# Four weight splits moved to GpSimd and one norm queued ahead of the other half's transposes, in a one-core decoder layer

## The chip, the cores and the metric

The kernel runs on one core of a Trainium2 chip. A core has TensorE (PE, with its weight loads shown as PEld), VectorE (DVE), ScalarE (ACT), GpSimd (POOL) and SyncE (SP, which here only starts loads). The metric is the device time of one execution in microseconds. A name like L73 is line 73 of the kernel.

## What is computed

One layer of a decoder trunk for 256 tokens of width 2048, in float32. A token mixer is followed by an output projection; then comes a gated MLP with a width-3 causal convolution. Both have an RMS norm before and behind them and are scaled and shifted by a conditioning vector. The change lies between the output projection `merged @ w_o` and the up-projection `h @ w_up`:

```python
def rms_norm(x, g):
    y = x * lax.rsqrt(jnp.mean(x * x, axis=-1, keepdims=True) + RMS_EPS)
    return y * g

y = hybrid_mixer(h, ...)                       # ends with  merged @ w_o
x = x + gt1[:, None] * rms_norm(y, g_post_mix)
h = rms_norm(x, g_pre_ffn) * (1.0 + sc2[:, None]) + sh2[:, None]
up = causal_dwconv(h @ w_up, ffn_conv_w)       # w_up: 2048 x 11264
a, b = jnp.split(up, 2, axis=-1)
y = (jax.nn.silu(a) * b) @ w_down
x = x + gt2[:, None] * rms_norm(y, g_post_ffn)
```

## The kernel before

Every product is made from split operands: a value becomes hi (its rounding to fp32r, the format that TensorE takes) and lo (the value less hi). `split` (L71) does this with a cast on ScalarE (L72) and a subtraction on VectorE (L73). Weights come as tiles of 128x1024 in a fixed order, `sources` (L85): `weights` (L75) starts the load of one tile into `raw` (4 buffers) and splits it into `hi` and `lo` (4 buffers each; the last two tiles of the output projection go to `dx` buffers). `next_weights` (L121) hands out a tile and keeps two more on the way. What is written to a buffer waits until the buffer's last reader is through.

The output projection is `out_proj` (L270). It makes four column blocks n of 512, for two token halves t of 128 tokens each. In the last block the last six weight tiles are held, so that all products of half 0 come first, then all of half 1. Behind each half stand its square sum on ScalarE (L299), the product with the gate on VectorE (L300), and then `tail(t)`, which here is `mid` (L850), in a high-priority section. After half 0 one tile of the up-projection is prefetched, after half 1 the next ones.

`mid(t)` has two steps. The norm: `rms_scale` (L262) sums the four partial sums (reduction L264, square root on ScalarE L265, reciprocal L266, three Newton operations L258 to L260, all on 128x1 values); four operations add the result to x (L855, 128x512 each), each followed by a square sum on ScalarE (L856); a second `rms_scale`; and then the identity matrix is scaled by the second norm into `dg` (L859). The transposes: for four blocks b, four products of x with `dg` (L864) turn 128x128 pieces into a PSUM tile `tps` (of four PSUM buffers), two of the four pieces are scaled and shifted from PSUM by VectorE (L872), two by ScalarE (L874), and two splits write `h2p`, the operand of the up-projection, hi and lo side by side.

The up-projection loops over 44 column tiles f, twice each (the halves a and b): 16 products of `hi` with both parts of `h2p` (L901) and 16 of `lo` with the hi part (L902). It needs all of `h2p`, tile after tile.

The order on each engine is made by a scheduler from the order of the code, the priorities and the waits; each engine then works through its own list in that order. In the kernel before, GpSimd has work in the first 130 us only.

Of the kernel before, what the change touches and what calls it, by code (L numbers as in the profile page):

```python
# [49 lines left out]
def kernel(  # L50
# [3 lines left out]
    nc = tc.nc  # L54
    wmod_h = (wmod_h0, wmod_h1)
    wmod_t = (wmod_t0, wmod_t1)
    pool = lambda n, bufs=1, **kw: ctx.enter_context(tc.tile_pool(name=n, bufs=bufs, **kw))
# [6 lines left out]
    def raw_tile(src):  # L64
        t = sp.tile([P, 1024], F32, tag="raw", name="raw", bufs=4)
        nc.sync.dma_start(t, src)
        return t
# [3 lines left out]
    def split(src, hi, lo):  # L71
        marks["act"] = nc.scalar.copy(hi, src)  # L72
        nc.vector.tensor_sub(lo, src, hi)  # L73

    def weights(src, pool=None):  # L75
        r = raw_tile(src)
        if pool is None:
            h = sp.tile([P, 1024], F32R, tag="hi", name="hi", bufs=4)
            l = sp.tile([P, 1024], F32R, tag="lo", name="lo", bufs=4)
        else:  # L80
            h, l = (pool.tile([P, 1024], F32R, tag="dx", name="dx", bufs=5) for _ in range(2))
        split(r, h, l)
        return h, l

    def sources():  # L85
        for grp in GROUPS:
            for b in range(10):
                for g in grp:
                    yield wA[b, g], None
        for i in range(4):  # L90
            for f in (4 + i, 8 + i, i):
                for j in range(2):
                    yield wB[f, j], None
        for br in GATE_ORDER:
            for f in range(16):
                for j in range(2):
                    yield wB[12 + 16 * br + f, j], None
                if f % 2 == 0:
                    yield wbr[br, f // 2], None
        for n in range(4):  # L100
            for j in range(8):
                yield wo[n, j], marks["dx"] if n == 3 and j >= 6 else None
        for f in range(NF):
            for ft in (f, f + NF):
                for j in range(2):
                    yield wup[ft, j], None
        for n in range(4):
            for j in range(NF // 2):
                yield wdn[n, j], None

    queue = []
    stream = sources()

    def prefetch(n):
        while len(queue) < n:
            src = next(stream, None)
            if src is None:
                break
            queue.append(weights(*src))
# [137 lines left out]
    def newton(r, t, ms, n=1):  # L257
        nc.vector.scalar_tensor_tensor(t, r, -0.5 / n, r, ALU.mult, ALU.mult)  # L258
        nc.vector.scalar_tensor_tensor(ms, ms, EPS * n, t, ALU.add, ALU.mult)
        nc.vector.scalar_tensor_tensor(r, ms, 1.5, r, ALU.add, ALU.mult)  # L260

    def rms_scale(ss):  # L262
        v, t, r = (cp.tile([P, 1], F32, tag=n, name=n, bufs=2) for n in ("rv", "rt", "rr"))
        nc.vector.tensor_reduce(v, ss, AX.X, ALU.add)  # L264
        nc.scalar.activation(r, v, AF.Sqrt, bias=eps[:, 0:1], scale=1.0 / D)  # L265
        nc.vector.reciprocal(r, r)  # L266
        newton(r, t, v, D)
        return r
# [38 lines left out]
    with ExitStack() as mx:  # L307
# [275 lines left out]
        for gi, grp in enumerate(GROUPS):  # L583
# [3 lines left out]
            for b in range(10):  # L587
# [6 lines left out]
                for half in range(2):  # L594
                    ps = psA.tile([P, 2, S], F32, tag="A", name="inps")
                    if b < 7:
# [10 lines left out]
                        f = 0.125 if 1 <= b <= 3 else 1.0  # L607
                    else:
# [12 lines left out]
                        f = 1.0  # L621
# [39 lines left out]
        def glu(zp):  # L661
            gq, gqh, gql = ssm_st["g"]
            branch_tiles(0)
            wg = [weights(wglu[j]) for j in range(2)]
            for f in range(4):
                ps = psB.tile([P, 512], F32, tag="B", name="glups")
                for kt in range(4):
                    w = wg[kt // 2]
                    c = 512 * (kt % 2) + P * f
                    mm3(  # L670
                        ps[:, :S], w[0][:, c : c + P], w[1][:, c : c + P], gqh[:, kt], gql[:, kt],
                        kt == 0, kt == 3,
                    )
                sg = zp.tile([P, S], F32, tag="z", name="sg", bufs=2)
                nc.scalar.activation(
                    sg, ps[:, :S], AF.Sigmoid, bias=V[:, V_BGLU + f : V_BGLU + f + 1]
                )
                nc.vector.tensor_mul(sg, sg, gq[:, f])
                split(sg, bo_h[0][:, f], bo_l[0][:, f])
# [167 lines left out]
            pp.tile([P, 2, 2, S], F32R, tag="big", name="h2p", bufs=12) for _ in range(8)  # L847
        ]

        def mid(t):  # L850
            r = rms_scale(ss[:, t])
            s2 = cp.tile([P, 4], F32, tag="s2", name="s2", bufs=2)
            for n in range(4):
                y = yg1[n][:, t]
                nc.vector.scalar_tensor_tensor(x1[t][n], y, r[:, 0:1], x1[t][n], ALU.mult, ALU.add)  # L855
                nc.scalar.activation(y, x1[t][n], AF.Square, accum_out=s2[:, n : n + 1])  # L856
            r2 = rms_scale(s2)
            dg = mp.tile([P, P], F32, tag="uv", name="dg", bufs=20)
            nc.vector.tensor_scalar_mul(dg, ident, r2[:, 0:1])  # L859
            tk = slice(P * t, P * t + P)  # L860
            for b in range(4):
                ps = psB.tile([P, 4, P], F32, tag="B", name="tps")
                for i in range(4):
                    nc.tensor.matmul(  # L864
                        ps[:, i], x1[t][b][:, P * i : P * i + P], dg, start=True, stop=True
                    )
                h2 = mp.tile([P, 4, P], F32, tag="uv", name="h2", bufs=20)
                for i in range(4):
                    kt = 4 * b + i
                    sc, sh = scale2[:, kt : kt + 1], shift2[:, kt : kt + 1]  # L870
                    if i < 2:
                        nc.vector.tensor_scalar(h2[:, i], ps[:, i], sc, sh, ALU.mult, ALU.add)  # L872
                    else:
                        nc.scalar.activation(h2[:, i], ps[:, i], AF.Identity, bias=sh, scale=sc)  # L874
                for i in range(2):
                    hp = h2p[2 * b + i]
                    split(h2[:, 2 * i : 2 * i + 2], hp[:, :, 0, tk], hp[:, :, 1, tk])

        out_proj(
            KT // 2, lambda kt, tk: (mh[kt // 2][:, kt % 2, tk], ml[kt // 2][:, kt % 2, tk]),  # L880
            gg, ss, lambda n, t: yg1[n][:, t], mid, mg, 6,
        )

# [7 lines left out]
    for f in range(NF):  # L891
# [13 lines left out]
        for a in range(2):  # L905
            ft = f + NF * a
# [145 lines left out]
```

## Time and profile before

| | |
|---|---|
| runs | 1638.06, 1642.01, 1641.61 us; median 1641.61 |
| profiled execution | 1646.62 us, of which the span is 1644.6 |
| busy: PE, DVE, ACT, POOL | 1587.6 (97%), 1217.2 (74%), 814.7 (50%), 52.0 us (3%) |
| chain that ended last | PE 81%, DVE 8%, DMA 7%, ACT 3% |
| up-projection | from 892.2 us; PE busy throughout 900 to 1380 us |
| turn to the up-projection | last product of the output projection starts at 875.9 us |

Times in the rows are counted from the start of the span. A busy time is the sum of an engine's operations; an operation's start and its length are the first two columns of a timeline. The profiled execution is one single run, 5.0 us above the median; sums made from its rows are carried over to the median as differences.

### The profile page before, as it was taken

What the parts mean: (1) busy time and instruction counts of PE and PEld (TensorE: products, weight loads), DVE (VectorE), ACT (ScalarE), POOL (GpSimd) and SP (SyncE); (2) the same over time, 40 slices, a digit from 0 to 9 for tenths busy, and PEclk for the clock granted to TensorE, in tenths of its full rate; (3) what the DMA queues carried; (4) which work ended last, traced back from release to release, by engine and by line L of the source; (5) the groups of instructions that cost most, each with busy time, mean ns of one, the idle gap of its engine ahead of it and who ended that gap; (6) DMA issues with size and microseconds to landing.
All of it is one profiled execution on the core that took longest, in us unless ns stands there. A gap on an engine that the chain in (4) does not pass through costs nothing.

```text
span 1644.6 us, 26089 instructions
## 1 busy us (share of the span) xinstructions
PE 1587.6 (97%) x10112; PEld 1400.8 (85%) x10112; DVE 1217.2 (74%) x1854; ACT 814.7 (50%) x1223; POOL 52.0 (3%) x102
## 2 busy tenths in 40 slices
PE   5899999999999999999998999999999999999997
PEld 3898998889888889999887888888888888888886
DVE  5889987887777788787757778877788777444444
ACT  4553434664445554544446555555555555343342
POOL 8021000000000000000000000000000000000000
PEclk8899999999999999999999999999999999999999
DMA  7988975777776665888864777767777665556563
GB/s 264 367 316 281 372 264 172 252 252 251 266 269 240 211 230 165 299 304 321 291 200 137 227 238 235 232 215 231 235 236 230 201 190 188 185 191 191 187 188 125
DMA packets 107120, 388.52 MB, mean 236 GB/s; under 512 B 11890, under 2 KB 12018, under 8 KB 106996
## 3 DMA queue, kind: packets, MB, share of 16 engines
q1 hardware_dynamic: 105268, 380.96, 69.5%
q10 hardware_dynamic: 1728, 5.90, 1.0%
q8 instruction: 79, 1.29, 0.3%
q14 instruction: 45, 0.37, 0.1%
HBM read 384.71 MB, written 2.10 MB: 235 GB/s over the span
## 4 chain that ended last, share of the span: by engine, by line
PE 81%; DVE 8%; DMA 7%; ACT 3%; issue 2%; SPq 0%; DVEq 0%; ACTq 0%
PE ups L901 20%; PE ups L902 10%; PE ops L127 7%; PE ops L126 7%; PE ops L128 7%; PE gps L126 5%; PE gps L128 5%; PE gps L127 5%; PE inps L126 4%; PE inps L128 4%; PE inps L127 4%; DVE lo L73 3%; DMA raw<-in_wB 2%; DMA raw<-in_wmod_t 2%; DMA raw<-in_wA 1%
## 5 line engine op out<-in xcount | busy, mean ns | idle before, releaser
L73 DVE TENSOR_TENSOR lo<-raw,hi 128x1024 fp32r<-128x1024 f32 x520 | 635.4, 1225 | 290.1 <-ACT hi L72 287.8
L72 ACT CAST hi<-raw 128x1024 fp32r<-128x1024 f32 x520 | 543.0, 1047 | 555.2 <-PE ops L128 172.9
L901 PE MATMUL ups<-h2p,hi 128*128 128x512 f32 x1408 | 495.3, 394 | 0.1
L902 PE MATMUL ups<-h2p,lo 128*128 128x256 f32 x1408 | 398.1, 283 | 0.0
L901 PEld LDWEIGHTS ups<-h2p,hi 128*128 128x128 f32 x1408 | 264.4, 188 | 61.6 <-ACT hi L72 0.5
L902 PEld LDWEIGHTS ups<-h2p,lo 128*128 128x128 f32 x1408 | 264.7, 188 | 0.6 <-issue 0.5
L128 PE MATMUL gps<-hh,lo 128*128 128x256 f32 x768 | 217.2, 283 | 4.1 <-DVE lo L73 4.1
L126 PE MATMUL gps<-hh,hi 128*128 128x256 f32 x768 | 220.0, 286 | 0.2 <-ACT hi L72 0.2
L127 PE MATMUL gps<-hl,hi 128*128 128x256 f32 x768 | 216.8, 282 | 0.0
L126 PEld LDWEIGHTS gps<-hh,hi 128*128 128x128 f32 x768 | 145.5, 189 | 15.7 <-issue 8.9
L128 PEld LDWEIGHTS gps<-hh,lo 128*128 128x128 f32 x768 | 145.3, 189 | 4.9 <-DVE lo L73 4.9
L126 PE MATMUL inps<-hh,hi 128*128 128x256 f32 x448 | 128.1, 287 | 22.1 <-ACT hh L72 14.8
L127 PEld LDWEIGHTS gps<-hl,hi 128*128 128x128 f32 x768 | 145.4, 189 | 0.2 <-issue 0.2
L126 PE MATMUL ops<-hi,ah 128*128 128x512 f32 x352 | 138.9, 395 | 0.0
L127 PE MATMUL ops<-lo,ah 128*128 128x512 f32 x352 | 138.9, 395 | 0.0
L128 PE MATMUL ops<-hi,al 128*128 128x512 f32 x352 | 138.9, 395 | 0.0
L128 PE MATMUL inps<-hh,lo 128*128 128x256 f32 x448 | 128.2, 287 | 1.9 <-DVE lo L73 1.7
L127 PE MATMUL inps<-hl,hi 128*128 128x256 f32 x448 | 127.4, 285 | 0.3 <-DVE hl L73 0.3
L126 PEld LDWEIGHTS inps<-hh,hi 128*128 128x128 f32 x448 | 85.9, 193 | 22.9 <-ACT hh L72 15.2
L128 PEld LDWEIGHTS inps<-hh,lo 128*128 128x128 f32 x448 | 85.6, 191 | 3.2 <-DVE lo L73 3.1
L127 PEld LDWEIGHTS inps<-hl,hi 128*128 128x128 f32 x448 | 86.0, 192 | 0.8 <-DVE hl L73 0.6
L193 DVE SCALAR_TENSOR_TENSOR mraw<-mraw,cond_row 128x1024 f32<-128x1024 f32 x64 | 79.1, 1254 | 0.7 <-DMA mraw<-in_wmod_t 0.6
(248 smaller groups left out, 2325.8 us busy)
## 6 DMA issues: line engine op xcount, KB each, us to landing
raw<-in_wup SPq DMA_DIRECT2D x176, 512.0 KB, 4.2
raw<-in_wB SPq DMA_DIRECT2D x120, 512.0 KB, 4.6
raw<-in_wdn SPq DMA_DIRECT2D x88, 512.0 KB, 3.5
raw<-in_wA SPq DMA_DIRECT2D x80, 512.0 KB, 5.2
mraw<-in_wmod_t SPq DMA_DIRECT2D x64, 512.0 KB, 5.9
raw<-in_wmod_t SPq DMA_DIRECT2D x32, 512.0 KB, 4.8
dx<-in_wmod_g SPq DMA_DIRECT2D x32, 512.0 KB, 6.7
raw<-in_wo SPq DMA_DIRECT2D x32, 512.0 KB, 4.5
```

The costliest lines, as they stand in the source:

```text
L72: marks["act"] = nc.scalar.copy(hi, src)
L73: nc.vector.tensor_sub(lo, src, hi)
L126: nc.tensor.matmul(dst, wh, ah, start=first, stop=False)
L127: nc.tensor.matmul(dst, wh, al, start=False, stop=False)
L128: nc.tensor.matmul(dst, wl, ah, start=False, stop=last)
L193: nc.vector.scalar_tensor_tensor(w, w, 1.0, cond_row[kc], ALU.mult, ALU.mult, accum_out=mp2[:, q, kc : kc + 1])
L901: nc.tensor.matmul(ps, wh[:, c], hp, start=kt == 0, stop=False)
L902: nc.tensor.matmul(ps[:, 0], wl[:, c], hp[:, 0], start=False, stop=kt == KT - 1)
```

## The change

Two things change. First, the four weight tiles of the first step of the up-projection (f = 0) are marked in `sources`, and `weights` splits them on GpSimd: the cast and the subtraction both go to that engine, in place of ScalarE and VectorE. Second, `mid` is parted into `mid_norm` and `mid_turn`. Half 0 calls only its norm; half 1 calls its norm and then the transposes of half 0 and of half 1.

```diff
-    def weights(src, pool=None):
+    def weights(src, pool=None, beside=False):
...
-        split(r, h, l)
+        if beside:
+            nc.gpsimd.tensor_copy(h, r)
+            nc.gpsimd.tensor_sub(l, r, h)
+        else:
+            split(r, h, l)
...
-                    yield wup[ft, j], None
+                    yield wup[ft, j], None, f == 0
...
+        dgs = []
+
         def mid(t):
+            mid_norm(t)
+            if t == 1:
+                for k in range(2):
+                    mid_turn(k)
+
+        def mid_norm(t):
             r = rms_scale(ss[:, t])
...
             nc.vector.tensor_scalar_mul(dg, ident, r2[:, 0:1])
+            dgs.append(dg)
+
+        def mid_turn(t):
+            dg = dgs[t]
             tk = slice(P * t, P * t + P)
```

In the changed kernel the lines behind the first edit have moved: L126 to L128 are L130 to L132, L855 is L867, L859 is L871, L864 is L880, L872 is L888, L901 and L902 are L917 and L918. Three places show how the lists of the engines differ.

TensorE at the turn, before. `ops` are the sums of the output projection (the last six rows' weights lie in `dx`), `tps` the transposes: x_9061 and x_9063 are half 0, x_9065 and x_9067 half 1.

```order
L128 MATMUL ops<-dx,ml 128x512
L126 MATMUL ops<-dx,mh 128x512
L127 MATMUL ops<-dx,mh 128x512
L128 MATMUL ops<-dx,ml 128x512
L864 MATMUL tps<-dg,x_9061 128x128 x8
L864 MATMUL tps<-dg,x_9063 128x128 x8
L864 MATMUL tps<-dg,x_9065 128x128 x8
L864 MATMUL tps<-dg,x_9067 128x128 x8
L901 MATMUL ups<-h2p,hi 128x512
```

The same place in the changed kernel:

```order
L132 MATMUL ops<-dx,ml 128x512
L880 MATMUL tps<-dg,x_9061 128x128 x8
L880 MATMUL tps<-dg,x_9063 128x128 x8
L130 MATMUL ops<-dx,mh 128x512
L131 MATMUL ops<-dx,mh 128x512
L132 MATMUL ops<-dx,ml 128x512
L880 MATMUL tps<-dg,x_9065 128x128 x8
L880 MATMUL tps<-dg,x_9067 128x128 x8
L917 MATMUL ups<-h2p,hi 128x512
```

The last three products of half 1 have moved behind the 16 transposes of half 0.

VectorE from the first norm of half 0 on, before (`rv`, `rt` and `rr` are the 128x1 values of `rms_scale`, `yg` the gated output):

```order
L264 TENSOR_REDUCE rv<-ss_9060 128x1
L73 TENSOR_TENSOR lo<-raw,hi 128x1024
L266 RECIPROCAL rr<-rr 128x1
L258 SCALAR_TENSOR_TENSOR rt<-rr 128x1
L73 TENSOR_TENSOR lo<-raw,hi 128x1024
L259 SCALAR_TENSOR_TENSOR rv<-rv,rt 128x1
L260 SCALAR_TENSOR_TENSOR rr<-rv,rr 128x1
L73 TENSOR_TENSOR lo<-raw,hi 128x1024
L855 SCALAR_TENSOR_TENSOR x_9061<-yg_9069,rr,x_9061 128x512
```

VectorE in the changed kernel, from the last addition of half 1 to the first splits of the transposed pieces (h_9778 to h_9806 are half 0):

```order
L867 SCALAR_TENSOR_TENSOR x_9067<-yg_9072,rr,x_9067 128x512
L268 TENSOR_REDUCE rv<-s_9753 128x1
L270 RECIPROCAL rr<-rr 128x1
L262 SCALAR_TENSOR_TENSOR rt<-rr 128x1
L263 SCALAR_TENSOR_TENSOR rv<-rv,rt 128x1
L264 SCALAR_TENSOR_TENSOR rr<-rv,rr 128x1
L871 TENSOR_SCALAR dg<-ident,rr 128x128
L888 TENSOR_SCALAR h_9778<-tps,scale_76,shift_77 128x128 x2
L888 TENSOR_SCALAR h_9792<-tps,scale_76,shift_77 128x128 x2
L888 TENSOR_SCALAR h_9806<-tps,scale_76,shift_77 128x128 x2
L73 TENSOR_TENSOR h2p<-h_9778,h2p 128x2x128 x2
```

The four subtractions of weight tiles have left this list, and all evictions of half 0 stand behind the whole norm of half 1; before, those of half 0 stood among the operations of half 1's second `rms_scale`. ScalarE's list has changed in the same way.

GpSimd at the end of its list in the changed kernel, where the list of before ends with its first row here (as L393):

```order
L397 TENSOR_TENSOR CQ<-CQ,tq 128x512
L83 CAST hi<-raw 128x1024
L84 TENSOR_TENSOR lo<-raw,hi 128x1024
L83 CAST hi<-raw 128x1024 x2
L84 TENSOR_TENSOR lo<-raw,hi 128x1024 x2
L83 CAST hi<-raw 128x1024
L84 TENSOR_TENSOR lo<-raw,hi 128x1024
```

Eight operations have been added. The list of loads on SP has the same rows as before; four of its loads now wait for GpSimd to leave a `raw` buffer, where they waited for VectorE.

## Rows read from the trace of the kernel before

**Rows 1.** Busy times in 900 to 1380 us; and one group of the page.

```profile
900.00:1380.00 480.00, 480.00 (x2725) 419.20 (x2724) 376.15 (x544) 267.57 (x425) 0.00 (x0) 1.00 0.70 223
...
L73 DVE TENSOR_TENSOR lo<-raw,hi 128x1024 fp32r<-128x1024 f32 x520 | 635.4, 1225 | 290.1 <-ACT hi L72 287.8
```

**Rows 2.** Timeline of TensorE at the turn: start us, length us, operation.

```profile
867.71 0.39 PE L128 MATMUL ops<-dx,ml 128*128 128x512 f32 x1
...
875.19 0.39 PE L128 MATMUL ops<-dx,ml 128*128 128x512 f32 x1
...
875.87 0.39 PE L128 MATMUL ops<-dx,ml 128*128 128x512 f32 x1
880.56 6.76 PE L864 MATMUL tps<-dg,x 128*128 128x128 f32 x32 [4.30 <-DVE dg L859]
888.31 3.81 PE L864 MATMUL tps<-dg,x 128*128 128x128 f32 x32 [0.99 <-issue]
892.21 0.50 PE L901 MATMUL ups<-h2p,hi 128*128 128x512 f32 x1
```

**Rows 3.** Half microseconds at the turn; the granted clock is third from the right.

```profile
879.50:880.00 0.50, 0.00 (x0) 0.00 (x0) 0.47 (x5) 0.09 (x1) 0.00 (x0) 0.89 0.98 82
...
886.50:887.00 0.50, 0.50 (x5) 0.50 (x5) 0.50 (x4) 0.49 (x2) 0.00 (x0) 0.79 0.00 0
```

**Rows 4.** Timeline of VectorE: the norms of both halves.

```profile
869.52 0.14 DVE L264 TENSOR_REDUCE rv<-ss 128x1 f32<-128x4 f32 x1
870.58 1.23 DVE L73 TENSOR_TENSOR lo<-raw,hi 128x1024 fp32r<-128x1024 f32 x1 [0.91 <-ACT hi L72]
...
874.55 2.73 DVE L855 SCALAR_TENSOR_TENSOR x<-yg,rr,x 128x512 f32<-128x512 f32 x4
...
878.93 0.15 DVE L264 TENSOR_REDUCE rv<-s 128x1 f32<-128x4 f32 x1
...
879.44 0.16 DVE L266 RECIPROCAL rr<-rr 128x1 f32<-128x1 f32 x1 [0.30 <-ACT rr L265]
...
880.22 0.29 DVE L859 TENSOR_SCALAR dg<-ident,rr 128x128 f32<-128x128 f32 x1
...
880.61 2.74 DVE L855 SCALAR_TENSOR_TENSOR x<-yg,rr,x 128x512 f32<-128x512 f32 x4
...
884.14 0.16 DVE L264 TENSOR_REDUCE rv<-s 128x1 f32<-128x4 f32 x1
...
887.93 0.28 DVE L859 TENSOR_SCALAR dg<-ident,rr 128x128 f32<-128x128 f32 x1
```

**Rows 5.** Timelines of ScalarE and VectorE: two evictions each.

```profile
889.29 0.81 ACT L874 ACTIVATE h<-tps,shift,scale 128x128 f32<-128x128 f32 x2
...
890.59 0.81 ACT L874 ACTIVATE h<-tps,shift,scale 128x128 f32<-128x128 f32 x2
...
892.41 0.72 DVE L872 TENSOR_SCALAR h<-tps,scale,shift 128x128 f32<-128x128 f32 x2
893.05 0.75 DVE L73 TENSOR_TENSOR h2p<-h,h2p 128x256 fp32r<-128x256 f32 x2
```

**Rows 6.** Timelines of VectorE and GpSimd early in the kernel, 114 to 126 us.

```profile
114.51 3.58 DVE L73 TENSOR_TENSOR lo<-raw,hi 128x1024 fp32r<-128x1024 f32 x2 [0.40 <-ACT hi L72]
118.01 0.68 DVE L625 SCALAR_TENSOR_TENSOR uqk<-inps,uqk 128x512 f32<-128x512 f32 x1
...
122.25 3.17 DVE L73 TENSOR_TENSOR lo<-raw,hi 128x1024 fp32r<-128x1024 f32 x2
...
114.98 2.03 POOL L387 TENSOR_TENSOR tq<-CT,fi 128x512 f32<-128x512 f32 x1
...
123.64 1.58 POOL L389 TENSOR_SCALAR CQ<-CQ 128x512 f32<-128x512 f32 x1
125.19 1.14 POOL L391 TENSOR_TENSOR tq<-CT,fr 128x512 f32<-128x512 f32 x1
```

**Rows 7.** Timeline of GpSimd: a memset and a subtraction of 128x128.

```profile
0.80 0.53 POOL L402 MEMSET condp<- 128x512 f32 x1
...
31.65 0.45 POOL L373 TENSOR_TENSOR SC<-SC,ta 128x128 f32<-128x128 f32 x1
```

## Prediction

> **What bounds the kernel now.** First the stages: over the up-projection, which follows the place of the change, TensorE is busy for all 480.00 us of the 480 looked at, at clock 1.00 [rows 1]. Whatever moves the start of that stage therefore moves the end of the kernel by as much. Then the turn from the output projection to the up-projection, on TensorE [rows 2]: the last product of the first token half starts at 867.71 and ends at 868.10, the last of the second half starts at 875.87. TensorE then has nothing until the first half's 16 transposes at 880.56 (6.76 us), the second half's follow at 888.31 (3.81 us), and the first up-projection product starts at 892.21. In the idle stretch the granted clock falls from 1.00 to 0.50, at about 879.9, some 3.6 us after the last product, and comes back between 886.5 and 887.0, about 6.1 us after the transposes began [rows 3]. That is why equal sets of transposes take 6.76 and 3.81 us.
>
> What TensorE waits for is the norm on VectorE and ScalarE [rows 4]: the first half's sums are added up at 869.52, but its four additions to x start only at 874.55, since weight splits (one at 870.58) stand between; the scaled identity dg of the first half starts at 880.22 and lasts 0.29 us (to 880.51), the second half's ends at 888.21. The change works on just these steps.
>
> **Part 1: the splits leave the norm.** Alone, the norm of a half is a chain that rows 4 give piece by piece. From the last product's end to the reduction 1.42 us (868.10 to 869.52). From a reduction to the reciprocal 0.51 (878.93 to 879.44), and from there to the operation behind the Newton steps 0.78 (879.44 to 880.22): 1.29 together. From the first addition to x to the next reduction 3.53 (880.61 to 884.14). From that reduction to the end of dg 1.58 (878.93 to 880.51). Sum 7.82 us. With no split in between, the first dg is done at 868.10 + 7.82 = 875.92 and not at 880.51: a gain of 4.6 us at this point, if nothing else slows VectorE.
>
> **Part 2: GpSimd takes the splits.** Its eight operations (four casts, four subtractions of 128x1024) are not in the trace, so they are bounded. Subtraction: 1.14 us for 512 elements and 0.45 for 128 [rows 6, 7] give 1.14 + 512 x 0.69/384 = 2.06 for 1024, or 2.28 by doubling; I take 2.1. Cast: two one-input operations of 512 elements cost a pair of VectorE subtractions 3.17 - 2.38 = 0.8 us, so 0.4 each and 0.8 for 1024; doubling the memset's 0.53 gives 1.06, doubling the contended 1.58 gives 3.2 [rows 6, 7]. I take 1.0, nearest to the memset. By themselves these 12.4 us would hide: the first product that needs one comes after 892.
>
> They do not run by themselves. Where GpSimd works beside VectorE, two VectorE subtractions from SBUF take 3.58 us in place of 2.38 (1.23 for one [rows 1] and about 1.15 for one that follows directly), and GpSimd's 512-element operation 2.03 in place of 1.14, while a VectorE operation that reads PSUM keeps its 0.68 [rows 6]. The lengthened ends fall on the other engine's ends: GpSimd's begins at 114.98 and ends at 117.01, the second subtraction ends at 118.09. The two engines take turns, one whole operation each. The Trainium skill, page "SBUF — State Buffer", section "SBUF: two separate sides", says of this pair of ports that it is "an exclusive lock, not a bandwidth split", for VectorE operations with two SBUF inputs too; the trace agrees, by these rows, and by that rule the time is the 1659 below, while a split of bandwidth would leave it nearer to the second rival's 1646.
>
> So between each two of VectorE's norm operations with two SBUF inputs one GpSimd operation gets in. VectorE's are three Newton steps, four additions to x, three Newton steps; GpSimd's are cast, subtraction, cast, cast, subtraction, subtraction, cast, subtraction, from about 869.4, when the first hi buffer comes free (the second half's first six products, 0.23 us each, have passed since 868.0). The first cast still has 0.2 us to go when the first Newton step is ready; the next six operations each stand before one VectorE operation: 2.1 + 1.0 + 1.0 + 2.1 + 2.1 + 1.0 = 9.3; of the last subtraction 1.5 us are covered by the last square, the reduction and the square root, 0.6 are not. Sum 10.1 us. First dg at 875.92 + 10.1 = 886.0: the 4.6 us gained turn into 5.5 lost.
>
> **Part 3: the order.** On TensorE the 16 transposes of the first half now stand ahead of the last three products of the second half, which need nothing that is late. So the second half's norm can't start before the first half's dg and transposes are through. TensorE waits from about 875.4 (where the product after the one at 875.19 would start) to 886.05, long enough by rows 3 for the clock to fall: transposes 6.76 us, three products 0.68 and the drain of the last 0.17, to 893.65. Then the second half's chain, 7.82 us, without GpSimd, which is done by about 885: second dg at 901.5, against 888.21.
>
> Third, on VectorE and ScalarE the first half's evictions stand behind the second half's whole norm; before, they ran beside it (ScalarE's for the first half began ahead of the second dg). The four PSUM buffers of the transposes are all held by the first half until then. The first comes free after a VectorE pair of 0.72 and a ScalarE pair of 0.81 [rows 5], with hand-overs 1.65 us after dg; TensorE has by then idled since 893.65, more than the 3.6 us of rows 3, so the second set costs 6.76 again: first up-projection product 8.4 us after the second dg. The evictions set a floor below that: ScalarE goes through a tile each 1.30 us (889.29, 890.59 [rows 5]), VectorE through 0.72 + 0.75 and alike; the first tile of the second half is the fifth, 0.8 + 4 x 1.30 + 1.2 + 0.4 = 7.6 us after dg. Before it was 892.21 - 888.21 = 4.0 us.
>
> **Sum.** First up-projection product at 901.5 + 8.4 = 909.9 against 892.21: 17.7 us later. In parts: first dg +5.5, from it to the second dg 15.5 in place of 7.7 (+7.8), from there to the first product +4.4. Loads and the rest of the up-projection are as before: the SP queue has the same rows, four weight loads now wait for GpSimd, whose last subtraction is through by about 885, before the stage they feed has begun. The profiled execution took 1646.62 us (span 1644.6), 5.0 above the median of 1641.61; on it the sum is 1664.3, on the median **1659.3**.
>
> **Rivals.**
> (1) Only the 512-element additions give way, while the short Newton steps (some 0.2 us apart) pass ahead of a waiting GpSimd. For it: no row of this trace has three such steps in a row beside large GpSimd work. Then 0.2, then the subtraction and both casts and a subtraction before the four additions, 6.2, and 0.6 after them: 7.0 us in place of 10.1. The clock still falls. +14.6, or 1656.2.
> (2) Not slower by what can be measured: GpSimd alone waits and the norm runs free. First dg at 875.92, TensorE idle for 0.6 us only, so the clock stays and the transposes take 3.81; three products to 880.6; second dg 888.4; first product 7.6 to 8.4 later, 896.0 to 896.8. That is +3.8 to +4.6, or 1645.4 to 1646.2: the turned order costs as much as the splits gave back. Against it stand the rows 6. It decides from the point where VectorE's additions keep their 2.73 us for four beside a busy GpSimd. Even with the three products ahead of the transposes, the second dg would be at 876.26 + 7.82 = 884.1 and the first product at 891.7 to 892.5, no gain: the evictions queued behind the norm take it.
> (3) Longer casts, up to the 3.2 us bound: 2.2 more for each of four casts and 0.7 for the subtractions at 2.28, up to +9.5 on top, 1664 to 1669.
>
> **Chances.** Forecast 0.65, (1) 0.13, (2) 0.12, (3) 0.10. The forecast's own bounds (cast 0.8, subtraction 2.06: one less) give 1658 to 1662. The range 1650 to 1667 leaves out (2) and about half of (3). A measurement of this kernel tells about 0.3%, 4.9 us, from no change: (2) is "same" with 0.10; 0.02 is left for faster, for which no row speaks; slower 0.88.
>
> **What would show it.** Eight GpSimd rows from about 869.4 to 885, the subtractions well above 2.1 us where VectorE stands between; the four additions to x of the first half over some 9 us, not 2.73; first transposes at about 886 at clock 0.50; three output products behind them; second dg at about 901.5; second transposes near 903, again at 0.50; first up-projection product near 910; nothing else moved. Wrong: additions of the first half within 3 us (rival 2), Newton steps close together but the additions apart (rival 1), or second transposes at full clock (up to 0.8 less).

## The result, and the profile after

The changed kernel takes 1657.75 us (median of 4 runs, 1652.58 to 1659.73) against 1641.81 for the kernel before (4 runs beside it): ratio 1.0094, 95% interval [1.0069, 1.0119], slower by 15.9 us. Run again later it took 1657.90 against 1643.06, ratio 1.0087 [1.0059, 1.0114].

The profiled execution of the changed kernel took 1658.04 us, its span is 1656.3. All that follows is counted from one event, the end of the last output product of the first token half: 868.10 in the kernel before [rows 2], 863.88 + 0.39 = 864.27 here. First TensorE at the turn (timeline of the changed kernel: start us, length us, operation, and in brackets the idle time before it and what ended it). L132 is the output product, L880 the transposes, L917 the up-projection:

```profile
863.88 0.39 PE L132 MATMUL ops<-dx,ml 128*128 128x512 f32 x1
...
871.36 0.39 PE L132 MATMUL ops<-dx,ml 128*128 128x512 f32 x1
881.79 5.86 PE L880 MATMUL tps<-dg,x 128*128 128x128 f32 x32 [10.04 <-DVE dg L871]
...
887.95 0.40 PE L132 MATMUL ops<-dx,ml 128*128 128x512 f32 x1
897.71 6.41 PE L880 MATMUL tps<-dg,x 128*128 128x128 f32 x32 [9.36 <-ACT h L890]
903.87 0.48 PE L917 MATMUL ups<-h2p,hi 128*128 128x512 f32 x1
```

Against [rows 2] there are two idle stretches of 10.04 and 9.36 us where there was one of 4.30 and one of 0.99; the last three output products stand between the two sets of transposes (887.95 is the last of them); and both sets are slow, 5.86 and 6.41, where the second one had 3.81.

Where the first wait comes from is seen on VectorE and GpSimd (timelines of the same stretch). L262 to L264 are the Newton steps, L867 the additions to x, L871 builds dg, L83 and L84 are the casts and subtractions that GpSimd now does:

```profile
866.40 0.35 DVE L262 SCALAR_TENSOR_TENSOR rt<-rr 128x1 f32<-128x1 f32 x1
866.79 0.16 DVE L263 SCALAR_TENSOR_TENSOR rv<-rv,rt 128x1 f32<-128x1 f32 x1
866.98 2.25 DVE L264 SCALAR_TENSOR_TENSOR rr<-rv,rr 128x1 f32<-128x1 f32 x1
869.27 8.43 DVE L867 SCALAR_TENSOR_TENSOR x<-yg,rr,x 128x512 f32<-128x512 f32 x4
878.48 0.16 DVE L268 TENSOR_REDUCE rv<-s 128x1 f32<-128x4 f32 x1 [0.79 <-ACT yg L868]
879.00 0.16 DVE L270 RECIPROCAL rr<-rr 128x1 f32<-128x1 f32 x1 [0.36 <-ACT rr L269]
879.20 1.83 DVE L262 SCALAR_TENSOR_TENSOR rt<-rr 128x1 f32<-128x1 f32 x1
881.06 0.16 DVE L263 SCALAR_TENSOR_TENSOR rv<-rv,rt 128x1 f32<-128x1 f32 x1
...
881.45 0.28 DVE L871 TENSOR_SCALAR dg<-ident,rr 128x128 f32<-128x128 f32 x1
...
891.06 2.74 DVE L867 SCALAR_TENSOR_TENSOR x<-yg,rr,x 128x512 f32<-128x512 f32 x4
...
895.89 0.29 DVE L871 TENSOR_SCALAR dg<-ident,rr 128x128 f32<-128x128 f32 x1
```

```profile
865.70 1.04 POOL L83 CAST hi<-raw 128x1024 fp32r<-128x1024 f32 x1 [737.90 <-PE ops L132]
866.82 2.40 POOL L84 TENSOR_TENSOR lo<-raw,hi 128x1024 fp32r<-128x1024 f32 x1
869.16 2.49 POOL L83 CAST hi<-raw 128x1024 fp32r<-128x1024 f32 x2
871.62 5.53 POOL L84 TENSOR_TENSOR lo<-raw,hi 128x1024 fp32r<-128x1024 f32 x2
877.09 1.50 POOL L83 CAST hi<-raw 128x1024 fp32r<-128x1024 f32 x1
878.67 2.34 POOL L84 TENSOR_TENSOR lo<-raw,hi 128x1024 fp32r<-128x1024 f32 x1
```

A Newton step on one column lasts 0.16 us when nothing is in its way. The one at 866.98 lasts 2.25: it ends at 869.23, when GpSimd's first subtraction (866.82 + 2.40 = 869.22) ends. The one at 879.20 ends at 881.03, the last subtraction at 881.01. The four additions take 8.43 in place of 2.73 [rows 4], beside two casts and two subtractions. The same four additions of the second half, at 891.06, when GpSimd is done, take 2.74. The extra on these four rows is 0.19 + 2.09 + 5.70 + 1.67 = 9.65 us.

The granted clock (windows of the changed kernel; the clock is third from the right, TensorE's busy time stands behind the length of the window):

```profile
875.50:876.00 0.50, 0.00 (x0) 0.00 (x0) 0.50 (x1) 0.20 (x2) 0.50 (x1) 0.82 0.05 16
876.00:876.50 0.50, 0.00 (x0) 0.00 (x0) 0.50 (x1) 0.00 (x0) 0.50 (x1) 0.50 0.60 246
...
886.00:887.00 1.00, 1.00 (x10) 1.00 (x10) 0.00 (x0) 0.00 (x0) 0.00 (x0) 0.97 0.00 0
...
892.00:893.00 1.00, 0.00 (x0) 0.00 (x0) 1.00 (x2) 1.00 (x3) 0.00 (x0) 0.94 0.00 0
...
903.00:904.00 1.00, 1.00 (x10) 1.00 (x10) 0.79 (x3) 1.00 (x4) 0.00 (x0) 0.94 0.00 0
...
900.00:1380.00 480.00, 480.00 (x2724) 419.66 (x2724) 377.62 (x556) 270.58 (x440) 0.00 (x0) 1.00 0.71 221
```

It falls from 1.00 to 0.50 (of its two levels, from 2.4 to 1.2 GHz) twice, at about 875.8 and 892.9, once in each of the idle stretches, and comes back at about 886.1 and 903.1, in the middle of the transposes that follow. Behind the first up-projection product nothing has changed: 480.00 us busy of 480 at clock 1.00 as in [rows 1], and from that product to the end of the span 1656.3 - 903.87 = 752.43 us, before 1644.6 - 892.21 = 752.39.

So the whole difference sits between the two events. Counted from the end of the first half's last output product, in us:

| | first dg done | second dg done | first up-projection product |
|---|---|---|---|
| before | 12.41 | 20.11 | 24.11 |
| forecast for the change | 17.9 | 33.4 | 41.8 |
| changed | 17.46 | 31.91 | 39.60 |

### The profile page after: what moved, and what is told of

The parts are those of the page before. It is cut to its first block, busy times and chain, and to the rows that moved or that the text cites. A ratio compares the mean times of both kernels' runs of the same rounds, so it can differ in the third digit from the quotient of the medians.

```text
span 1656.3 us, 26085 instructions
## 1 busy us (share of the span) xinstructions
PE 1589.2 (96%) x10112; PEld 1403.0 (85%) x10112; DVE 1222.5 (74%) x1850; ACT 810.9 (49%) x1219; POOL 69.6 (4%) x110
## 4 chain that ended last, share of the span: by engine, by line
PE 81%; DVE 9%; DMA 6%; ACT 2%; issue 2%; SPq 0%; DVEq 0%; ACTq 0%
PE ups L917 20%; PE ups L918 10%; PE ops L131 7%; PE ops L130 7%; PE ops L132 7%; PE gps L130 6%; PE gps L132 6%; PE gps L131 6%; PE inps L130 4%; PE inps L132 4%; PE inps L131 4%; DVE lo L73 2%; DMA raw<-in_wB 2%; DMA raw<-in_wmod_t 2%; DMA raw<-in_wA 1%
## 5 line engine op out<-in xcount | busy, mean ns | idle before, releaser
L73 DVE TENSOR_TENSOR lo<-raw,hi 128x1024 fp32r<-128x1024 f32 x516 | 630.8, 1226 | 289.3 <-ACT hi L72 284.6
L917 PE MATMUL ups<-h2p,hi 128*128 128x512 f32 x1408 | 495.3, 394 | 0.0
L918 PE MATMUL ups<-h2p,lo 128*128 128x256 f32 x1408 | 398.0, 283 | 0.0
L917 PEld LDWEIGHTS ups<-h2p,hi 128*128 128x128 f32 x1408 | 264.4, 188 | 61.4 <-ACT hi L72 0.5
L918 PEld LDWEIGHTS ups<-h2p,lo 128*128 128x128 f32 x1408 | 264.7, 188 | 0.6 <-issue 0.5
L130 PE MATMUL gps<-hh,hi 128*128 128x256 f32 x768 | 219.8, 286 | 0.0
L132 PE MATMUL gps<-hh,lo 128*128 128x256 f32 x768 | 216.8, 282 | 2.6 <-DVE lo L73 2.6
L130 PEld LDWEIGHTS gps<-hh,hi 128*128 128x128 f32 x768 | 145.2, 189 | 15.9 <-issue 8.6
L130 PE MATMUL inps<-hh,hi 128*128 128x256 f32 x448 | 128.1, 287 | 20.6 <-ACT hh L72 13.6
L132 PEld LDWEIGHTS gps<-hh,lo 128*128 128x128 f32 x768 | 145.0, 189 | 3.1 <-DVE lo L73 3.0
L130 PE MATMUL ops<-hi,ah 128*128 128x512 f32 x352 | 138.9, 395 | 0.0
L132 PE MATMUL ops<-hi,al 128*128 128x512 f32 x352 | 138.9, 395 | 0.0
L132 PE MATMUL inps<-hh,lo 128*128 128x256 f32 x448 | 128.8, 288 | 1.9 <-DVE lo L73 1.7
L130 PEld LDWEIGHTS inps<-hh,hi 128*128 128x128 f32 x448 | 86.3, 194 | 21.4 <-ACT hh L72 14.0
L132 PEld LDWEIGHTS inps<-hh,lo 128*128 128x128 f32 x448 | 86.2, 193 | 3.1 <-DVE lo L73 3.1
L130 PEld LDWEIGHTS ops<-hi,ah 128*128 128x128 f32 x352 | 66.3, 188 | 15.6
```

The source lines that it names most:

```text
L130: nc.tensor.matmul(dst, wh, ah, start=first, stop=False)
L132: nc.tensor.matmul(dst, wl, ah, start=False, stop=last)
L917: nc.tensor.matmul(ps, wh[:, c], hp, start=kt == 0, stop=False)
L918: nc.tensor.matmul(ps[:, 0], wl[:, c], hp[:, 0], start=False, stop=kt == KT - 1)
```

## Experiments

The theory: VectorE's norm and GpSimd's splits take turns, one whole operation each, so that the first dg comes some 10 us later than the norm alone would give it (5 us later than before); the output products that stand behind the first transposes hand this delay on to the second half; the idle stretches make the transposes run at half clock. Rivals: VectorE keeps its pace and the turned order is the cost; or VectorE waits for all of GpSimd's work. Each kernel below is told in the same three milestones (first dg, second dg, first up-projection product), since in all ten profiles the rest of the program takes the same 752.4 us.

### Each half of the change alone

The kernel before with the splits on GpSimd, and the code of the norm in its old order:

```diff
+        if beside:
+            nc.gpsimd.tensor_copy(h, r)
+            nc.gpsimd.tensor_sub(l, r, h)
+        else:
+            split(r, h, l)
...
-                    yield wup[ft, j], None
+                    yield wup[ft, j], None, f == 0
```

> Only the four splits on GpSimd; the norm and the transposes in the order of before (each half's evictions right behind its own dg). In this build TensorE still has the last three products of half 1 behind the transposes of half 0. Counted from the end of half 0's last product, the first up-projection product came after 24.1 us in the kernel before and after 39.6 in the changed one. Turns theory (each GpSimd operation that reads SBUF gets one whole turn between two VectorE operations with two SBUF inputs): first dg as in the changed kernel, 17.5; second dg near 32.6, since the evictions of half 0 now stand ahead of parts of half 1's norm; second transposes again at half clock; first up-projection product at about 39, so about +15 us on the kernel before, the same as the changed kernel. Rival (the queued order of the norm makes the loss, GpSimd costs little): first dg near 8, first product near 24 to 26, within 2 us of the kernel before.

Measured: milestones 17.48, 32.65, 37.81; 1658.09 us, ratio 1.0104 [1.0087, 1.0121]. TensorE, as above (L868 the transposes, L905 the up-projection):

```profile
865.46 0.39 PE L132 MATMUL ops<-dx,ml 128*128 128x512 f32 x1
...
883.38 6.07 PE L868 MATMUL tps<-dg,x 128*128 128x128 f32 x32 [10.05 <-DVE dg L863]
889.75 0.40 PE L132 MATMUL ops<-dx,ml 128*128 128x512 f32 x1
898.60 5.32 PE L868 MATMUL tps<-dg,x 128*128 128x128 f32 x32 [8.45 <-issue]
903.66 0.48 PE L905 MATMUL ups<-h2p,hi 128*128 128x512 f32 x1
```

The 10.05 us of idle time are there without the second half of the change, and the three products stand behind the first transposes here too: it isn't the new order of the code that puts them there, but the splits leaving VectorE and ScalarE.

The changed kernel with those splits back on ScalarE and VectorE, so that only the order of the norms is new:

```diff
-                    yield wup[ft, j], None, f == 0
+                    yield wup[ft, j], None
```

> Only the new order of norm and transposes; the splits stay on ScalarE and VectorE. In this build TensorE has all products of half 1 ahead of the transposes, as before. Turns theory: first dg as before, 12.4 us after half 0's last product; second dg earlier than before, at 17.6 in place of 20.1, because no eviction stands in the norm; but all evictions behind it, 7.6 us to the first up-projection product: 25.2 in place of 24.1. +1 us, no difference that can be measured. Rival (the order makes the loss): +8 us or more.

Measured: 12.40, 17.62, 25.20; 1643.08 us, ratio 1.0016 [1.0003, 1.0029]. As expected: the second dg comes 2.5 us earlier, since no eviction stands between its steps, and the evictions behind it take that back and 1.1 us more. The first up-projection product waits for a split behind them (L73):

```profile
884.97 0.50 PE L917 MATMUL ups<-h2p,hi 128*128 128x512 f32 x1 [0.91 <-DVE h2p L73]
```

### GpSimd's place taken by writes

The changed kernel, with GpSimd writing zeros to the eight tiles in place of splitting; it neither reads nor computes:

```diff
-            nc.gpsimd.tensor_copy(h, r)
-            nc.gpsimd.tensor_sub(l, r, h)
+            nc.gpsimd.memset(h.bitcast(F32), 0.0)
+            nc.gpsimd.memset(l.bitcast(F32), 0.0)
```

> The changed kernel, but GpSimd writes zeros to hi and lo of the four tiles in place of splitting them (so the first step of the up-projection is wrong): eight GpSimd operations on the same buffers, none of which reads SBUF; TensorE's order is that of the changed kernel. Turns theory, with turns only against operations that read SBUF: the norm runs alone, first dg 7.8 us after half 0's last product, TensorE idle for under 1 us so the first transposes run at full clock (under 4.5 us in place of 5.9), second dg at 20.4, first up-projection product at about 28: +4 us on the kernel before, 11 to 12 less than the changed kernel. Rival (GpSimd's writes cost VectorE as much as its reads): eight operations of about 1 us between VectorE's, first dg at 13 to 15, first product 34 to 37.

Measured: 8.50, 20.92, 28.62; 1646.78 us, ratio 1.0038 [1.0019, 1.0058]. VectorE's steps of the first half, then GpSimd's last write, then TensorE (timelines of this kernel):

```profile
866.51 0.16 DVE L264 SCALAR_TENSOR_TENSOR rr<-rv,rr 128x1 f32<-128x1 f32 x1
866.71 2.74 DVE L867 SCALAR_TENSOR_TENSOR x<-yg,rr,x 128x512 f32<-128x512 f32 x4
...
871.54 0.95 DVE L871 TENSOR_SCALAR dg<-ident,rr 128x128 f32<-128x128 f32 x1
```

```profile
871.46 0.96 POOL L84 MEMSET lo<- 128x1024 f32 x1
```

```profile
872.55 3.84 PE L880 MATMUL tps<-dg,x 128*128 128x128 f32 x32 [1.08 <-DVE dg L871]
876.68 0.40 PE L132 MATMUL ops<-dx,ml 128*128 128x512 f32 x1
886.45 6.41 PE L880 MATMUL tps<-dg,x 128*128 128x128 f32 x32 [9.37 <-ACT h L890]
```

GpSimd's writes last from 865.19 to 872.42, through the whole norm, but the Newton steps and the additions keep their 0.16 and 2.74. So what costs is not that GpSimd is busy, nor that it writes. The run takes its reading from SBUF and its arithmetic away together, and does not tell the two apart. One step does wait, the one that builds dg: 0.95 us in place of 0.29, until the write that began at 871.46 is through. With the delay gone TensorE idles 1.08 us, the granted clock stays at 1.00, and the first transposes take 3.84. The order of TensorE is still that of the changed kernel, and the second wait (9.37) is still there.

### The products ahead of the transposes

The changed kernel, with both halves' transposes queued behind the last output products:

```diff
             mid_norm(t)
-            if t == 1:
-                for k in range(2):
-                    mid_turn(k)
...
+        for k in range(2):
+            mid_turn(k)
```

> The changed kernel with the transposes of both halves called after the output projection and outside its high-priority section: GpSimd's splits and VectorE's and ScalarE's lists are as in the changed kernel, but on TensorE the last three products of half 1 are ahead of all transposes again. Turns theory: first dg as in the changed kernel, 17.5 us after half 0's last product; half 1's sums are ready then, so its dg follows 7 us later, at 24.4 in place of 31.9; TensorE is idle for under 3 us before the second transposes, so they keep the full clock; first up-projection product at 32 in place of 39.6: +8 us on the kernel before. Rival (the place of the three products matters little, the turns make all of it): first product at 38 or later.

Measured: 17.47, 24.39, 32.06; 1652.92 us, ratio 1.0071 [1.0056, 1.0086]. The second dg is 7.5 us earlier than in the changed kernel, and the second wait of TensorE falls from 9.36 to 2.76. This is the price of the products' place. TensorE's rows (L877 the transposes, those of the second half now in pieces, L916 the up-projection), and the granted clock over that stretch:

```profile
893.51 1.16 PE L877 MATMUL tps<-dg,x 128*128 128x128 f32 x8 [2.76 <-ACT h L887]
...
899.59 0.48 PE L916 MATMUL ups<-h2p,hi 128*128 128x512 f32 x1 [0.99 <-DVE h2p L73]
```

```profile
893.50:899.60 6.10, 4.65 (x33) 3.92 (x33) 5.65 (x18) 6.10 (x20) 0.00 (x0) 1.00 0.01 3
```

The second set runs at full clock here, and yet the first up-projection product comes 7.67 us after the second dg, as in the changed kernel with its second set at half clock (7.69): it waits for the evictions. So the half clock of the second set costs next to nothing by itself.

Both at once, zeros from GpSimd and the products ahead:

> The changed kernel with both of its costs taken away: GpSimd only writes zeros where it would split (so the split of the first four weight tiles is left out, and the first step of the up-projection is computed with zeros), and the three last products of the second half stand ahead of all transposes again; the evictions of both halves stay queued behind the second half's norm. It tests the sentence of the prediction that even so there would be no gain. Counted from the end of the first half's last product. Theory: first dg at about 8.2 to 8.5 (the run with zeros had 8.50), TensorE idle for well under 1 us, so the first transposes run at full clock, 3.8; the second half's chain begins at its own last product, 8.16, and its dg is at 8.16 + 7.8 = 16.0; the evictions of the first half wait for that, so the first up-projection product is 7.6 to 8.4 later, at 23.6 to 24.4. That is 0.5 less to 0.3 more than the 24.1 of the kernel before: about 1641 us, ratio 0.999 to 1.001. Rival: the evictions find gaps between the norm's operations, and the first product comes at about 16.0 + 4.0 = 20, which is 4 us earlier: 1637, ratio 0.9975.

Measured: 8.50, 15.98, 23.66; 1641.31 us, ratio 0.9989 [0.9974, 1.0004]. The rival, a first up-projection product at 20, falls: between the second dg and it there are 7.68 us, as in the changed kernel (7.69), where the kernel before has 4.00, because all evictions stand behind the second half's norm. The two rows (L868 builds dg):

```profile
879.84 0.28 DVE L868 TENSOR_SCALAR dg<-ident,rr 128x128 f32<-128x128 f32 x1
```

```profile
887.80 0.47 PE L916 MATMUL ups<-h2p,hi 128*128 128x512 f32 x1 [0.37 <-DVE h2p L73]
```

With the evictions in their new place, splits that cost nothing and products ahead of all transposes are together worth 0.45 us by the trace, which can't be told from nothing.

These kernels make a ladder for the first up-projection product: 24.11 before; 23.66 with free splits and the products ahead; 28.62 with the products behind the first transposes (+4.96); 39.60 with real splits on GpSimd (+10.98). Taken the other way round the splits cost 8.40 (23.66 to 32.06) and the products' place 7.54 (32.06 to 39.60): the two costs raise each other by 2.58. Of this, 2.02 are the clock of the first transposes (5.86 at half clock, 3.84 at full), which the second half pays for only where its products stand behind them; the other 0.56 are slack: with free splits and the products ahead, the second half's norm waits for its own last products and not for the first dg.

The kernel before with zeros from GpSimd, its norm in the old order:

> GpSimd only writes zeros where it would split the first four weight tiles (so that split is left out, and the first step of the up-projection is computed with zeros), and the code of the norm stands as it did before: the most that could come from taking the splits off VectorE and ScalarE at no price. Counted from the end of the first half's last product; the kernel before has its first dg at 12.4 and its first up-projection product at 24.1. Theory: first dg at 8.2 to 8.5, transposes at full clock, 3.8; the second half's three products stand behind them and end at about 13, so the second dg is at about 13 + 7.8 = 20.8, and the first product is 4.0 to 4.2 later, 24.8 to 25: as late as before or up to 1 us later, ratio 0.9995 to 1.001. Rival: the splits are what the turn costs; the 4 us gained at the first dg reach the first product, at about 20, and the time is 4 us less, 1637.5.

Measured: 8.49, 21.49, 26.62; 1645.87 us, ratio 1.0016 [1.0001, 1.0032]. The rival's 20 is far off, and the theory's 24.8 to 25 was missed by 1.6. TensorE's rows (L868 the transposes, L905 the up-projection) show what it left out:

```profile
873.31 0.40 PE L132 MATMUL ops<-dx,ml 128*128 128x512 f32 x1
882.21 5.27 PE L868 MATMUL tps<-dg,x 128*128 128x128 f32 x32 [8.50 <-issue]
887.24 0.48 PE L905 MATMUL ups<-h2p,hi 128*128 128x512 f32 x1
```

TensorE idles 8.50 us behind the three products, so the second transposes run at half clock, 5.27 in place of 3.8; and the second dg came 0.7 later than summed up, of which 0.6 are evictions of the first half that get between the steps of its norm. In this order of TensorE, then, taking the splits off VectorE and ScalarE doesn't pay: even at no price the first up-projection product comes 2.5 us later than before. That it could not pay in any order is not shown: no kernel here has free splits, the products ahead of the transposes and each half's evictions right behind its own dg, all three at once.

### Each subtraction made twice

The changed kernel with twelve GpSimd operations in place of eight:

```diff
             nc.gpsimd.tensor_sub(l, r, h)
+            nc.gpsimd.tensor_sub(l, r, h)
```

> The changed kernel with each of GpSimd's four subtractions made twice: twelve GpSimd operations in place of eight, same result. It tells how VectorE's norm waits. Counted from the end of the first half's last product; in the changed kernel the first dg was at 17.5, the first up-projection product at 39.6. Theory (turns, one whole operation each): what gets in ahead of the first dg is set by how many two-input operations VectorE has there, three Newton steps, four additions, three Newton steps; more of the operations that get in are subtractions, and the three last Newton steps, which met only one GpSimd operation, meet up to three more: first dg 3.5 to 5.5 us later, 21 to 23, the first product at about 43 to 45, the time about 1662. Rival 1, VectorE waits until GpSimd's whole queue is through: four subtractions of 2.1 to 2.4 us more, 8.4 to 9.6 us, first dg at 26 to 27, time about 1667. Rival 2, the port isn't the cause and the extra work hides on GpSimd: first dg at 17.5, no difference to the changed kernel.

Measured: 21.29, 35.24, 42.84; 1660.26 us, ratio 1.0107 [1.0079, 1.0135]. The norm's steps on VectorE, and GpSimd's last operations (L85 is the added subtraction, L868 the additions, L872 builds dg):

```profile
864.70 2.25 DVE L265 SCALAR_TENSOR_TENSOR rr<-rv,rr 128x1 f32<-128x1 f32 x1
866.98 8.44 DVE L868 SCALAR_TENSOR_TENSOR x<-yg,rr,x 128x512 f32<-128x512 f32 x4
...
876.93 0.71 DVE L263 SCALAR_TENSOR_TENSOR rt<-rr 128x1 f32<-128x1 f32 x1
877.67 2.26 DVE L264 SCALAR_TENSOR_TENSOR rv<-rv,rt 128x1 f32<-128x1 f32 x1
879.97 0.94 DVE L265 SCALAR_TENSOR_TENSOR rr<-rv,rr 128x1 f32<-128x1 f32 x1
880.95 2.33 DVE L872 TENSOR_SCALAR dg<-ident,rr 128x128 f32<-128x128 f32 x1
```

```profile
880.87 2.33 POOL L85 TENSOR_TENSOR lo<-raw,hi 128x1024 fp32r<-128x1024 f32 x1
883.16 2.35 POOL L84 TENSOR_TENSOR lo<-raw,hi 128x1024 fp32r<-128x1024 f32 x1
885.59 2.35 POOL L85 TENSOR_TENSOR lo<-raw,hi 128x1024 fp32r<-128x1024 f32 x1
```

The first dg is 3.8 us later than in the changed kernel, within the 3.5 to 5.5 of the theory. GpSimd has 9.4 us more to do (four times 2.35), and its queue ends at 887.94, well after dg at 883.28: VectorE did not wait for the queue to end (rival 1), and it did not run free (rival 2). The four additions take the same 8.44 with more work queued on the other side: each gets its turn after one operation. The last steps, which met one GpSimd operation in the changed kernel, now meet four, and one of them is the build of dg, which begins 0.08 us after a subtraction and ends 0.08 us after its end. The first up-projection product, 3.2 us later, is just below the 43 to 45 expected (the transposes took 5.37), and the time 2.4 us above that of the changed kernel on the same chip.

### The place of the first event itself

> The changed kernel once more, on the same chip as the other three, for the place of its time: 39.6 from the end of the first half's last product to the first up-projection product, and 752.4 from there to the end, as in its first profile. What is open is the time of that last product itself, 864.3 in the first profile where the kernel before had 868.1 on an identical program up to there. If that is a difference from run to run, it comes at another time in this profile, anywhere between 860 and 868; if the build sets it, at 864 again. Ratio 1.007 to 1.012.

Measured: 17.45, 32.10, 39.91, and 1659.6 - 907.25 = 752.35 from there to the end. The event from which all is counted came at 867.34 in this profile, at 864.27 in the other one of the same kernel. So its time is not set by the build; it differs from run to run. In the ten profiles of all the kernels it lies between 859.8 and 868.1. With 792 us behind it, the eight spans of the changed kernel (1650.8 to 1659.6) put it anywhere between 859 and 868, if the rest is as fixed in every run as in the two profiles. That bounds what the medians can say. The milestones of the kernels with the splits alone (+13.7 over before) and with the products ahead (+8.0) are each some 3 us less than their medians (+16.8 and +11.6); that of the kernel with each subtraction twice (+18.7) is 1.5 us more than its median (+17.2). The difference lies ahead of the first event, where the programs do the same work; four runs of each don't tell whether it is the same spread or something of those kernels. It stays open.

## Why the prediction was right

Forecast +17.7 us and 1659.3; measured 1657.75, +15.9, by the two traces +15.5 at the first up-projection product. The time is inside the range of 1650 to 1667, though just below the 1658 to 1662 of the forecast's own bounds, and it lies as near to rival 1's 1656.2 as to the forecast: not the time but the rows on VectorE and GpSimd decide between the two.

- **What bounds it.** Right: the up-projection is busy throughout, and what delays its start is found at the end. 752.43 against 752.39.
- **The norm's chain alone, 7.82.** Right: the second half's, undisturbed, takes 7.83 (888.35 to 896.18). The first half with zeros takes 8.50, of which 0.66 are the one wait of dg.
- **Turns, 10.1.** Measured 9.65, and the mechanism is as told: the Newton steps give way as the additions do (rival 1 is refuted by 2.25 and 1.83 us for 0.16), and rival 2 by 8.43 for the additions. The rows that it was read from [rows 6] show two subtractions only as one length, so that "one whole operation each" was an inference then. Term by term: first cast 0.2, measured 0.19; first subtraction 2.1, measured 2.09, but on the third Newton step, since the second one (866.79) passed in the gap of 0.08 us between cast and subtraction; two casts and two subtractions ahead of the additions 6.2, measured 5.70; fourth cast 1.0, measured 0, since it (877.09) lay beside the last square and the reduction; last subtraction 0.6, measured 1.67, since it began that much later. The last two errors belong together and nearly cancel: the stretch between the last addition and the next Newton step hides some of GpSimd's work, and it hid the cast in place of most of the subtraction. The sizes: a cast, taken as 1.0, lasts 1.04; a subtraction, taken as 2.1 with bounds of 2.06 and 2.28, lasts 2.35 alone, above both, but made a step wait 2.09 only.
- **First dg, +5.5.** Measured 17.46 - 12.41 = +5.05; the 0.45 less are from the turns.
- **First to second dg, 15.5.** Measured 14.45 = 0.06 + 5.86 (transposes) + 0.70 (three products) + 7.83. The order of the pieces and all of them but one were right; the transposes were put at the 6.76 of [rows 2]. The clock came back 4.3 us after they had begun, against 6.1 in [rows 3].
- **Second dg to the first product, 8.4.** Measured 7.69: 1.53 to the first free PSUM buffer, where 1.65 was summed up, and the transposes 6.16 to the first product in place of 6.76. The releaser of that wait is ScalarE's eviction (ACT h L890 on the row at 897.71), as said. The floor of 7.6 that the evictions set was right too: with the second set at full clock it took 7.58 and 7.67 (order alone, products ahead), so the set, with its 6.16 in place of 6.76, hardly reaches past that floor.
- **Rival 3**, longer casts, fell with the 1.04; the sentence that even with the products ahead the splits would give nothing back was tested as such: 23.66 against 24.11.

The mis-sized term is thus one row used twice: the 6.76 of a set that starts at half clock. The fourteen such sets in the profiles of all kernels lasted 5.27 to 6.76. One reading, the longest of them as it turned out, stood for a thing that depends on when the clock returns; of the 2.2 us by which the sum was too long, 0.9 and 0.6 are from there and 0.45 from the turns.

One attribution was wrong, though no number of the sum hung on it. The prediction put the place of the three products behind the first transposes under the new order of the norms. The splits alone put them there too (first experiment), with the norms in the old order, while the new order alone leaves them ahead (second experiment: their last one starts at 867.53, the transposes at 872.23). And the place weighs more than the text lets one see: taken back by itself it returns 7.54 of the 15.5 us.

## What to carry to other kernels

An idle engine is not a free one: before handing work to GpSimd, look whether VectorE's chain on the critical path reads two inputs from SBUF at that time, and charge about one whole GpSimd operation for each such step that finds one queued, however short the step is (the build of dg, with one input tensor, gave way too). Large GpSimd operations are worst, since a step of 0.16 us then waits 2 us. And look on every engine for what the new order pushes behind a wait: three output products that needed nothing late, set behind the first transposes, make 7.54 of the 15.5 us lost.

## What the runs showed of the hardware

- **Not activity alone.** Beside GpSimd's casts and subtractions four additions took 8.43 us, beside its writes of zeros 2.74, the same as with GpSimd idle. The build of dg, with one tensor from SBUF, waits for both: 0.95 beside a write, 2.33 beside a subtraction, 0.29 alone. In the changed kernel the reduction at 878.48 and the reciprocal at 879.00 kept their 0.16 beside a cast and a subtraction. The Trainium skill, page "SBUF — State Buffer", section "Who interferes with whom", makes the same cut: an operation with two SBUF inputs contends with a GpSimd operation that reads, not with one that only writes, and a one-input tensor_scalar contends if it runs in a two-port mode. The runs agree on the first two points; in which mode the build of dg runs no run shows, only that it waits for both. The prediction had used only the first of the three.
- **The clock's return is not one number.** The granted 1.00 came back 4.3 and 5.4 us after the transposes had begun in the changed kernel, 6.1 in the kernel before; it fell about 4.1 and 4.5 us after the last product, before 3.6. Over the fourteen sets that began at half clock, in ten profiles, it came back about 3.1 to 6.2 us after the set had begun, and had fallen about 2.3 to 4.8 us after the last product or transpose; with the products ahead, an idle stretch of 2.76 us kept it.
- **A spread ahead of the turn**, on work that doesn't differ: 864.27 and 867.34 in two profiles of one kernel, 859.8 to 868.1 in the ten profiles; over the eight runs of the changed kernel some 9 us, if the rest is as fixed as in the profiles.
